# One layer of gated attention, one of window attention: full-width operands, moved copies and moved squares

## The chip, the cores and the metric

The kernel runs on one core of a Trainium2 chip. Its engines are TensorE (PE, matrix products; PEld is its load of weights), VectorE (DVE), ScalarE (ACT), GpSimd (POOL) and SyncE (SP, which only issues transfers). Each has its own instruction stream; they meet at semaphores. DMA queues are fed by SP and ACT (hardware queues) and by POOL (a software queue). The metric is the device time in microseconds of one execution, the median of the runs shown.

## What is computed

One inference step of a decoder of two layers for two groups of requests that share the weights: a prompt of 1024 tokens and 8 samples of 8 tokens, so 1088 token columns of 1024 features. Layer 0 mixes tokens with gated linear attention (four heads, keys of 128, values of 256 features), layer 1 with attention over a window of 128 positions, a bias table and past keys and values. Each layer then has an MLP with squared ReLU and a gated embedding:

```python
def step(state, inp):                       # linear attention, per head and chunk
    bc = jnp.cumsum(lc, axis=-2)            # lc = log_sigmoid(a @ w_a2 + b_a2) / 16
    attn = jnp.einsum('bhid,bhjd,bhijd->bhij', qc, kc, decay)
    o = (jnp.einsum('bhij,bhje->bhie', attn, vc)
         + jnp.einsum('bhid,bhde->bhie', qc * jnp.exp(bc), state))
    new_state = (jnp.exp(last)[..., None] * state
                 + jnp.einsum('bhjd,bhje->bhde', kc * jnp.exp(last - bc), vc))
...
h = h + gla_or_swa(rmsnorm(h, w['norm_mix'][i]))
h = h + jnp.square(jax.nn.relu(rmsnorm(h, w['norm_mlp'][i]) @ w_up)) @ w_down
gate = jax.nn.sigmoid(rmsnorm(h, w['norm_ple'][i]) @ w['w_ple_gate'][i])
h = h + gate * (p[i] @ w['w_ple'][i])
```

Outputs are the final activations, the new states of the linear attention and the key and value caches of the window (for the samples: the old cache moved on by eight positions).

## The kernel before

Activations lie with features on the 128 partitions and the 1088 tokens along the free dimension, in 8 tiles. Products run in three parts: weights and activations are split into a high part (rounded to fp32r) and the rest, and `mm3` (L163, L164, L165) adds high*high, high*rest and rest*high into one PSUM tile. Token columns come in three chunks (364, 362, 362), so one weight tile of 128x512 (four blocks of 128 features) serves 36 matmuls.

Weights come through `wfill`: a load into one of two `raw` buffers on SP's queue, a cast on ACT (L139, `whi`), a subtraction on DVE (L140, `wlo`), each into one of five buffers. `wnext` keeps this three tiles ahead of PE. `load()` (L77) issues on SP and chains every load behind the one before, so that SP's order is the order in which the program was written. The order on the other engines is set by a scheduler that goes by its own cost model and may put instructions of one engine in another order than they were written.

`gla_layer` first loads the eight input tiles x; per tile it makes the split (L195 on ACT, L196 on DVE) and sums the squares of x for the norm into `acc`: squares on ACT (L275) or POOL (L273), sums on DVE (L281, L283, L288) or POOL (L279). PE meanwhile multiplies tile after tile with the first head's q and k weights; then it sums `acc` over partitions (L231). After that the attention runs as a generator, `gla_steps`, over 4 heads x 9 chunks (8 of the prompt, one of the samples), with the projections of the next head filled in between its matmuls. The steps that the change touches:

- `gla_lg`: the gate's logarithm; L463 multiplies `aT` (17 rows: 16 features and a row of ones) with `wa2`, loaded anew for each head (17x128).
- `gla_scores`: scores of a chunk by levels of s = 64, 32, ..., 1; L534 takes `w-s` columns of E as weights, so 64 of them at s = 64 and 96 to 127 at the others. L536 and L537 follow.
- `gla_out`: L558, L563, L565 with full tiles.
- `gla_out_sample`: the samples' chunk; L594 multiplies `km` (masked keys, 64 rows) with `vs` (values, 64 rows), two passes for each of 8 samples' pairs, L599 multiplies `vs` with `ats` (64 rows).

An fp32 matmul shows as two passes in the trace (x2 for one matmul).

`bias_rows` at the layer's end makes 16 rows of 384 bias values in DRAM (`ed1`); `bias_copies` (L795, L798) spreads them to 16x128 rows (`ed`) in eight copies of 384 KB and copies the old caches (`kcs`, `vcs`, 960 KB each) to their place in the outputs. It is called at the start of each of the eight blocks (fb) of the first MLP. Its transfers are issued by POOL, where nothing else stands ahead of them, so that they start as soon as `ed1` is written, during the output projection of the attention (`out_proj`). `sample_bias` reads `ed` into `bs`, and the window attention reads both.

`out_proj` adds to each of its products the residual, which is loaded again from the input into one single buffer x (L659, on ACT's queue); the sum is DVE's (L640), then follow squares for the next norm (L225, L226) and splits. `mlp` runs over 8 blocks: four up tiles f (each of two weight tiles, three chunks; evacuated by L691 on DVE, L692 and L693 on ACT, L694 on DVE) and then eight down tiles.

Of the kernel before, what the change touches and what calls it, by code (L numbers as in the profile page):

```python
# [19 lines left out]
P = 128  # L20
D = 1024
KT = D // P
# [24 lines left out]
class Trunk:  # L47
# [204 lines left out]
    def gla_layer(self):  # L252
        nc, I, O = self.nc, self.I, self.O
        with ExitStack() as ctx:
# [4 lines left out]
            for k in range(KT):  # L259
                x = self.single()  # L260
                if k == 0:
                    self.wfill(1)
                for c0, cn in CH if k == 0 else ((0, T),):
                    self.load(x[:, c0:c0 + cn], I["xT"][k][:, c0:c0 + cn])
                self.wfill((2, 2, 2, 3, 4, 4, 5, 5)[k])
                self.split(hg[k], x, self.gain(G_MIX0, k), CH if k == 0 else ((0, T),))

                if k == 0:
                    nc.scalar.activation(self.acc[:, :T], x, AF.Square)
                    continue  # L270
                sq = self.double("G3", F32, [P, T])
                if k in (1, 4):
                    nc.gpsimd.tensor_tensor(sq, x, x, op=ALU.mult)  # L273
                elif k < KT - 1:
                    nc.scalar.activation(sq, x, AF.Square)  # L275
                if k == 1:
                    acc2 = sq
                elif k in (3, 4):
                    nc.gpsimd.tensor_tensor(acc2, acc2, sq, op=ALU.add)  # L279
                elif k < KT - 1:  # L280
                    nc.vector.tensor_tensor(self.acc[:, :T], self.acc[:, :T], sq, op=ALU.add)  # L281
                if k == 6:
                    nc.vector.tensor_tensor(self.acc[:, :T], self.acc[:, :T], acc2, op=ALU.add)  # L283
                if k == KT - 1:
                    for c0, cn in CH:
                        c = slice(c0, c0 + cn)
                        nc.scalar.activation(sq[:, c], x[:, c], AF.Square)
                        nc.vector.tensor_tensor(self.acc[:, c], self.acc[:, c], sq[:, c], op=ALU.add)  # L288
            self.norm_end(token_major=True)

            self.load(self.ident, I["ident"])
            self.load_wa2(0)
            tri = ga.tile([P, P], F32R, name="tri")
# [21 lines left out]
            for a in self.at:  # L315
                nc.gpsimd.memset(a, 0.0)
            self.ats = ga.tile([TS, TS], F32, name="ats")
            nc.gpsimd.memset(self.ats, 0.0)
# [35 lines left out]
    def gla_proj(self, h, hg):  # L354
# [26 lines left out]
        v = d["v"] = self.double("G3", F32, [P, 8, DV])  # L381
        vs = d["vs"] = self.ga.tile([TS, DV], F32, tag="vs", name=self.uid("vs"), bufs=1)
        wv = [self.wnext(("v", h, g)) for g in range(4)]
# [14 lines left out]
        if h == 0:  # L398
            aT = self.aT = self.rs.tile([P, TP], F32, tag="acc", name="aT", bufs=1)
            nc.gpsimd.memset(aT[:17, :], 1.0)  # L400
            for t0 in range(0, 9, 4):
# [51 lines left out]
    def gla_lg(self, h, c):  # L453

        nc, ga = self.nc, self.ga
        if c == 0:
            self.wa2 = self.wa2next
            if h + 1 < HEADS:
                self.load_wa2(h + 1)
        m, n = (P, 2) if c < 8 else (TS, 1)  # L460
        ps = self.ps("gs")
        for i in range(n):
            nc.tensor.matmul(ps[:m, i * P:(i + 1) * P], lhsT=self.aT[:17, (c + i) * P:(c + i) * P + m],  # L463
                             rhs=self.wa2, start=True, stop=True)
        w = n * P
# [10 lines left out]
                                                 for i in range(n)}}  # L476

    def load_wa2(self, h):
        self.wa2next = self.ga.tile([17, P], F32, tag="wa2", name=self.uid("wa2"), bufs=2)
        self.load(self.wa2next, self.I["wa2"][h])  # L480

# [40 lines left out]
    def gla_scores(self, h, c, pre):  # L522
# [8 lines left out]
        for l, s in enumerate(levels):  # L531
            ev = E[:, l, :].rearrange("p (n two s) -> p n two s", two=2, s=s)
            nc.vector.tensor_tensor(ev, ev, _dims(base, ([2 * s, w // (2 * s)], [T + s, 2], [1, s])), op=ALU.mult)
            nc.tensor.matmul(pp[:w - s, l * hw:(l + 1) * hw], lhsT=E[:, l, :w - s], rhs=ev[:, :, 1, :], start=True, stop=True)  # L534
        nc.vector.tensor_tensor(ke[:, :w], ke[:, :w], base, op=ALU.mult)
# [40 lines left out]
    def gla_out_sample(self, h, st):  # L576
        nc, ga, g, d = self.nc, self.ga, self.g, self.head[h]
        pp, pd, kt, qe, sm = st
        vs, o, tok = d["vs"], d["o"], SEQ
        self.gla_pick(self.ats, g["msks"], pp, pd, TS, LVS)  # L580
        pi = self.ps("gx")
        for b in range(NB):
            if b % 2 == 0:
                km = ga.tile([TS, 2, P], F32, tag="km", name=self.uid("km"), bufs=1)
                nc.vector.tensor_tensor(km, kt[:TS, :].unsqueeze(1).broadcast_to([TS, 2, P]),
                                        g["bmask"][:, b:b + 2].unsqueeze(2).broadcast_to([TS, 2, P]), op=ALU.mult)
                pu = self.ps("gs")
# [202 lines left out]
    def bias_copies(self, i):  # L790
# [3 lines left out]
        s = slice(2 * i, 2 * i + 2)  # L794
        r = self.nc.gpsimd.dma_start(self.ed[s], self.ed1[s].unsqueeze(1).broadcast_to([2, P, 384]))  # L795
        if i == FB - 1:
            for out, past in (("kcs", "kpast"), ("vcs", "vpast")):
                c = self.nc.gpsimd.dma_start(self.O[out][:, 0:120, :], self.I[past][:, 8:128, :])  # L798
                self.order(c.ins, r.ins)

# [450 lines left out]
```

## Time and profile before

| | before |
|---|---|
| median of 3 runs | 2784.34 us (2783.4 to 2785.63) |
| profiled execution | 2783.81 us |
| its span | 2782.0 us |
| PE busy | 2743.9 us, 99% |
| DVE / ACT / POOL busy | 52% / 38% / 5% |

The span is what the trace covers; a little lies around it. Matmuls are pipelined: their durations overlap, so the distance from start to start is what one costs. In a shape like 64*128 64x256 the first pair is the weights' rows and columns, the second the moving operand's rows and columns. What stands in brackets at a row's end is how long the engine was idle before it, and who ended that.

### The profile page before, as it was taken

Reading aid. Unit: us, or ns where it says so; the run is one execution under the profiler, and the core shown is the slowest. Engines: PE = TensorE matmul, PEld = TensorE weight load, DVE = VectorE, ACT = ScalarE, POOL = GpSimd, SP = SyncE. Lnnn points to the kernel's source line nnn. Section 1 sums busy time; section 2 is a strip of 40 time slices with the busy share of each in tenths; the row PEclk is TensorE's granted clock in tenths of the full one; section 3 lists DMA queues with packets and bytes.
Section 4 is the critical chain, followed back from the end, with each engine's and each line's share of the span. In section 5 each row is a group of like instructions: output and inputs, shape, how many; then the busy total and the mean of one; then the engine's idle time right before and its main releaser. Section 6 shows DMA issues by size and latency. Waiting matters only on the chain.

```text
span 2782.0 us, 43335 instructions
## 1 busy us (share of the span) xinstructions
PE 2743.9 (99%) x17265; PEld 2655.9 (95%) x17265; DVE 1455.3 (52%) x3479; ACT 1058.6 (38%) x2301; POOL 148.2 (5%) x166
## 2 busy tenths in 40 slices
PE   8999999999999999999999999999999999999997
PEld 8988988999999999999999988799999999999997
DVE  5766876543333333333756577654333333333687
ACT  4544655432221221122534566533222221221475
POOL 1000000040000000000000233200000000000000
PEclk9999999999999999999999999999999999999999
DMA  3111121341111111111122101121111111111053
GB/s 116 35 59 39 31 69 58 114 118 46 46 54 42 55 43 45 46 42 43 54 71 82 48 24 54 55 79 50 42 54 45 43 51 46 46 46 42 24 192 101
DMA packets 96322, 163.40 MB, mean 59 GB/s; under 512 B 16457, under 2 KB 33501, under 8 KB 96088
## 3 DMA queue, kind: packets, MB, share of 16 engines
q1 hardware_dynamic: 87448, 150.09, 17.8%
q0 software_dynamic: 7520, 6.09, 0.8%
q10 hardware_dynamic: 1152, 4.46, 0.5%
q8 instruction: 136, 2.23, 0.3%
q14 instruction: 66, 0.54, 0.1%
HBM read 145.94 MB, written 19.98 MB: 60 GB/s over the span
## 4 chain that ended last, share of the span: by engine, by line
PE 95%; DVE 2%; ACT 1%; DMA 1%; issue 1%; SPq 0%; POOL 0%; DVEq 0%; ACTq 0%; POOLq 0%
PE mm L163 21%; PE mm L164 21%; PE mm L165 21%; PE gx L165 7%; PE gx L164 7%; PE gx L163 7%; PE gx L534 2%; PE gx L1024 1%; PE gx L1010 1%; PE gs L594 1%; PE gx L563 1%; DMA x<-in_xT 1%; PE gx L558 1%; PE gs L993 1%; PE gx L592 0%
## 5 line engine op out<-in xcount | busy, mean ns | idle before, releaser
L163 PE MATMUL mm<-G,whi 128*128 128x362 f32 (+1 forms) x3416 | 1130.6, 331 | 6.6 <-ACT G L195 6.2
L164 PE MATMUL mm<-G,whi 128*128 128x362 f32 (+1 forms) x3416 | 1127.8, 330 | 2.4 <-DVE G L196 2.4
L165 PE MATMUL mm<-G,wlo 128*128 128x362 f32 (+1 forms) x3416 | 1126.7, 330 | 0.1
L163 PEld LDWEIGHTS mm<-G,whi 128*128 128x128 f32 x3416 | 642.8, 188 | 15.6 <-ACT G L195 6.5
L164 PEld LDWEIGHTS mm<-G,whi 128*128 128x128 f32 x3416 | 643.2, 188 | 9.0 <-issue 3.6
L165 PEld LDWEIGHTS mm<-G,wlo 128*128 128x128 f32 x3416 | 642.4, 188 | 5.8 <-issue 3.5
L139 ACT CAST whi<-raw 128x512 fp32r<-128x512 f32 (+1 forms) x368 | 226.8, 619 | 722.7 <-PE mm L164 702.9
L165 PE MATMUL gx<-G,wlo 128*128 128x362 f32 (+1 forms) x1048 | 343.6, 328 | 1.3 <-DVE wlo L140 1.3
L164 PE MATMUL gx<-G,whi 128*128 128x362 f32 (+1 forms) x1048 | 343.7, 328 | 0.0
L163 PE MATMUL gx<-G,whi 128*128 128x362 f32 (+1 forms) x1048 | 343.0, 328 | 0.0
L140 DVE TENSOR_TENSOR wlo<-raw,whi 128x512 fp32r<-128x512 f32 (+1 forms) x368 | 257.6, 702 | 68.1 <-ACT whi L139 67.2
L703 DVE TENSOR_TENSOR H<-H,mm 128x364 f32<-128x364 f32 (+1 forms) x256 | 136.2, 532 | 271.2 <-PE mm L165 269.9
L692 ACT ACTIVATE tmp<-tmp 128x362 f32<-128x362 f32 (+1 forms) x192 | 97.3, 508 | 392.6 <-DVE tmp L691 385.5
L165 PEld LDWEIGHTS gx<-G,wlo 128*128 128x128 f32 x1048 | 197.5, 188 | 1.8 <-DVE wlo L140 1.6
L163 PEld LDWEIGHTS gx<-G,whi 128*128 128x128 f32 x1048 | 197.5, 189 | 0.1
L164 PEld LDWEIGHTS gx<-G,whi 128*128 128x128 f32 x1048 | 197.3, 188 | 0.1
L694 DVE TENSOR_TENSOR G<-tmp,G 128x362 fp32r<-128x362 f32 (+1 forms) x192 | 102.9, 537 | 166.1 <-ACT G L693 166.1
L691 DVE SCALAR_TENSOR_TENSOR tmp<-mm,rb 128x364 f32<-128x364 f32 (+1 forms) x128 | 68.6, 536 | 178.4 <-PE mm L165 178.4
L703 DVE TENSOR_TENSOR H<-H,gx 128x362 f32<-128x362 f32 x128 | 68.0, 531 | 140.9 <-PE gx L165 140.9
L225 ACT ACTIVATE tmp<-H 128x362 f32<-128x362 f32 (+1 forms) x126 | 63.6, 506 | 143.8 <-DVE H L640 85.4
L925 POOL TENSOR_TENSOR G<-tmp,G 64x364 fp32r<-64x364 f32 (+2 forms) x48 | 45.0, 939 | 983.7 <-ACT G L924 976.2
L693 ACT CAST G<-tmp 128x362 fp32r<-128x362 f32 (+1 forms) x192 | 95.1, 496 | 5.9
(247 smaller groups left out, 3066.5 us busy)
## 6 DMA issues: line engine op xcount, KB each, us to landing
raw<-in_w_up SPq DMA_DIRECT2D x128, 256.0 KB, 2.6
raw<-in_w_down SPq DMA_DIRECT2D x128, 256.0 KB, 2.6
G<-in_w_gate SPq DMA_DIRECT2D x24, 512.0 KB, 3.6
raw<-in_w_o SPq DMA_DIRECT2D x32, 256.0 KB, 3.2
raw<-in_w_q SPq DMA_DIRECT2D x24, 256.0 KB, 2.7
x<-in_xT ACTq DMA_DIRECT2D x8, 544.0 KB, 6.6
hd<-H SPq DMA_DIRECT2D x8, 544.0 KB, 3.8
x<-hd SPq DMA_DIRECT2D x8, 544.0 KB, 3.6
```

The costliest lines, as they stand in the source:

```text
L139: nc.scalar.copy(hi[:, s], raw[:, s])
L140: nc.vector.tensor_tensor(lo[:, s], raw[:, s], hi[:, s].bitcast(F32), op=ALU.subtract)
L163: mm(out, lhsT=w[0], rhs=x[0], start=first, stop=False)
L164: mm(out, lhsT=w[0], rhs=x[1], start=False, stop=False)
L165: mm(out, lhsT=w[1], rhs=x[0], start=False, stop=last)
L225: nc.scalar.activation(sq[:, :cn], h[:, s], AF.Square)
L534: nc.tensor.matmul(pp[:w - s, l * hw:(l + 1) * hw], lhsT=E[:, l, :w - s], rhs=ev[:, :, 1, :], start=True, stop=True)
L691: nc.vector.scalar_tensor_tensor(t[:, :cn], ps, 0.0, rb[:, s], op0=ALU.max, op1=ALU.mult)
L692: nc.scalar.activation(t[:, :cn], t[:, :cn], AF.Square)
L693: nc.scalar.copy(u[:, 0, s], t[:, :cn])
L694: nc.vector.tensor_tensor(u[:, 1, s], t[:, :cn], u[:, 0, s].bitcast(F32), op=ALU.subtract)
L703: nc.vector.tensor_tensor(h[:, s], h[:, s], ps, op=ALU.add)
```

## The change

Three things are changed.

1. Operands of the linear attention get 128 rows. `wa2` is one tile of 128 rows for all heads, set to zero on POOL and loaded once in its first 17 rows; `aT` is set to one in all 128 rows; `vs`, `km` and `ats` are tiles of 128 rows that are set to zero once, and later writes go to their first 64 rows. So L463, L594 and L599 contract over 128 rows. In `gla_scores` the weights of a level with 64 columns become w columns (128 at s = 64 of the prompt's chunks, 64 in the samples' chunk).
2. The copies of `bias_copies` are issued by `load()`, on SP's queue, in the order of the loads.
3. In the start the squares of all input tiles are ACT's, and their sums are DVE's.

```diff
@@ gla_layer
-                if k in (1, 4):
-                    nc.gpsimd.tensor_tensor(sq, x, x, op=ALU.mult)
-                elif k < KT - 1:
+                if k < KT - 1:
                     nc.scalar.activation(sq, x, AF.Square)
-                if k == 1:
-                    acc2 = sq
-                elif k in (3, 4):
-                    nc.gpsimd.tensor_tensor(acc2, acc2, sq, op=ALU.add)
-                elif k < KT - 1:
                     nc.vector.tensor_tensor(self.acc[:, :T], self.acc[:, :T], sq, op=ALU.add)
-                if k == 6:
-                    nc.vector.tensor_tensor(self.acc[:, :T], self.acc[:, :T], acc2, op=ALU.add)
...
-            self.load_wa2(0)
+            self.wa2 = ga.tile([P, HEADS, P], F32, name="wa2")
+            nc.gpsimd.memset(self.wa2, 0.0)
+            self.load(self.wa2[:17], I["wa2"].rearrange("h r c -> r h c"))
+            self.vs = ga.tile([P, DV], F32, name="vs")
+            self.km = ga.tile([P, 2, P], F32, name="km")
+            nc.gpsimd.memset(self.vs, 0.0)
+            nc.gpsimd.memset(self.km, 0.0)
...
-            self.ats = ga.tile([TS, TS], F32, name="ats")
+            self.ats = ga.tile([P, TS], F32, name="ats")
@@ gla_proj
-        vs = d["vs"] = self.ga.tile([TS, DV], F32, tag="vs", name=self.uid("vs"), bufs=1)
+        vs = self.vs[:TS]
...
-            nc.gpsimd.memset(aT[:17, :], 1.0)
+            nc.gpsimd.memset(aT, 1.0)
@@ gla_lg
-        if c == 0:
-            self.wa2 = self.wa2next
-            if h + 1 < HEADS:
-                self.load_wa2(h + 1)
...
-            nc.tensor.matmul(ps[:m, i * P:(i + 1) * P], lhsT=self.aT[:17, (c + i) * P:(c + i) * P + m],
-                             rhs=self.wa2, start=True, stop=True)
+            nc.tensor.matmul(ps[:m, i * P:(i + 1) * P], lhsT=self.aT[:, (c + i) * P:(c + i) * P + m],
+                             rhs=self.wa2[:, h, :], start=True, stop=True)
@@ gla_scores
-            nc.tensor.matmul(pp[:w - s, l * hw:(l + 1) * hw], lhsT=E[:, l, :w - s], rhs=ev[:, :, 1, :], start=True, stop=True)
+            m = w - s if w - s > 64 else w
+            nc.tensor.matmul(pp[:m, l * hw:(l + 1) * hw], lhsT=E[:, l, :m], rhs=ev[:, :, 1, :], start=True, stop=True)
@@ gla_out_sample
-        vs, o, tok = d["vs"], d["o"], SEQ
-        self.gla_pick(self.ats, g["msks"], pp, pd, TS, LVS)
+        vs, km, o, tok = self.vs, self.km, d["o"], SEQ
+        self.gla_pick(self.ats[:TS], g["msks"], pp, pd, TS, LVS)
...
-                km = ga.tile([TS, 2, P], F32, tag="km", name=self.uid("km"), bufs=1)
-                nc.vector.tensor_tensor(km, kt[:TS, :].unsqueeze(1).broadcast_to([TS, 2, P]),
+                nc.vector.tensor_tensor(km[:TS], kt[:TS, :].unsqueeze(1).broadcast_to([TS, 2, P]),
@@ bias_copies
-        r = self.nc.gpsimd.dma_start(self.ed[s], self.ed1[s].unsqueeze(1).broadcast_to([2, P, 384]))
+        self.load(self.ed[s], self.ed1[s].unsqueeze(1).broadcast_to([2, P, 384]))
...
-                c = self.nc.gpsimd.dma_start(self.O[out][:, 0:120, :], self.I[past][:, 8:128, :])
-                self.order(c.ins, r.ins)
+                self.load(self.O[out][:, 0:120, :], self.I[past][:, 8:128, :])
```

The order on the engines at three places. First DVE in the start, while PE multiplies the input tiles; G is the split of a tile where H is read, else a square. Before:

```order
L196 SCALAR_TENSOR_TENSOR G_85<-H_116,gains,G_85 128x1088
L196 SCALAR_TENSOR_TENSOR G_86<-H_122,gains,G_86 128x1088
L281 TENSOR_TENSOR acc_92<-acc_92,G_126 128x1088
L196 SCALAR_TENSOR_TENSOR G_87<-H_129,gains,G_87 128x1088
L140 TENSOR_TENSOR wlo_134<-raw_131,whi_133 128x512
L196 SCALAR_TENSOR_TENSOR G_88<-H_142,gains,G_88 128x1088
L140 TENSOR_TENSOR wlo_147<-raw_144,whi_146 128x512
L196 SCALAR_TENSOR_TENSOR G_89<-H_155,gains,G_89 128x1088
L281 TENSOR_TENSOR acc_92<-acc_92,G_159 128x1088
```

And now:

```order
L196 SCALAR_TENSOR_TENSOR G_85<-H_116,gains,G_85 128x1088
L273 TENSOR_TENSOR acc_92<-acc_92,G_120 128x1088
L196 SCALAR_TENSOR_TENSOR G_86<-H_123,gains,G_86 128x1088
L273 TENSOR_TENSOR acc_92<-acc_92,G_127 128x1088
L140 TENSOR_TENSOR wlo_135<-raw_132,whi_134 128x512
L196 SCALAR_TENSOR_TENSOR G_87<-H_130,gains,G_87 128x1088
L273 TENSOR_TENSOR acc_92<-acc_92,G_140 128x1088
L140 TENSOR_TENSOR wlo_148<-raw_145,whi_147 128x512
L196 SCALAR_TENSOR_TENSOR G_88<-H_143,gains,G_88 128x1088
L273 TENSOR_TENSOR acc_92<-acc_92,G_153 128x1088
```

Behind every split of a tile there stands now an addition (after's L273). Second, ACT in the first MLP at the end of a block's first up tile, whose three chunks are squared and cast by L692 and L693. Before:

```order
L139 CAST whi_7333<-raw_7331 128x512
L139 CAST whi_7382<-raw_7380 128x512
L139 CAST whi_7388<-raw_7386 128x512
L692 ACTIVATE tmp_7418<-tmp_7418 128x364
L693 CAST G_7392<-tmp_7418 128x364
L692 ACTIVATE tmp_7448<-tmp_7448 128x362
L693 CAST G_7392<-tmp_7448 128x362
L139 CAST whi_7485<-raw_7483 128x512
L139 CAST whi_7491<-raw_7489 128x512
L692 ACTIVATE tmp_7478<-tmp_7478 128x362
L693 CAST G_7392<-tmp_7478 128x362
```

And now, with those lines as L681 and L682:

```order
L139 CAST whi_7312<-raw_7310 128x512
L681 ACTIVATE tmp_7397<-tmp_7397 128x364
L682 CAST G_7371<-tmp_7397 128x364
L681 ACTIVATE tmp_7427<-tmp_7427 128x362
L682 CAST G_7371<-tmp_7427 128x362
L681 ACTIVATE tmp_7457<-tmp_7457 128x362
L682 CAST G_7371<-tmp_7457 128x362
L139 CAST whi_7361<-raw_7359 128x512
L139 CAST whi_7367<-raw_7365 128x512
L139 CAST whi_7464<-raw_7462 128x512
L139 CAST whi_7470<-raw_7468 128x512
```

The cast of the second up tile's second half (7382 before, 7361 now) has moved behind the three pairs. PE has moved with it: before it took both halves of the second tile chunk by chunk (24 matmuls each); now it takes the first half for all three chunks, 12 matmuls each, and then the second half. It is so in each of the eight blocks. Third, SP in the last block of the first MLP; before, only loads of weights stood there, and POOL had the copies, in this order:

```order
L785 DMA ed_5484<-rows 16x384
L795 DMA ed<-ed_5484 256x1x384 x8
L798 DMA out_kcs<-in_kpast 8x2x15360
L798 DMA out_vcs<-in_vpast 8x2x15360
L815 DMA bs<-ed 32x1x128
```

Now SP has:

```order
L77 DMA raw_12054<-in_w_up 128x512
L77 DMA raw_12102<-in_w_up 128x512
L77 DMA ed<-ed_5463 256x1x384
L77 DMA out_kcs<-in_kpast 8x2x15360
L77 DMA out_vcs<-in_vpast 8x2x15360
L77 DMA raw_12153<-in_w_up 128x512
L77 DMA raw_12159<-in_w_up 128x512
```

In the other seven blocks one copy of `ed` stands between two loads of up weights. Behind the first MLP the order of PE, ACT and DVE is as before.

## Rows read from the trace of the kernel before

**Rows 1.** The page, chain that ended last: shares of the span by engine.

```profile
PE 95%; DVE 2%; ACT 1%; DMA 1%; issue 1%; SPq 0%; POOL 0%; DVEq 0%; ACTq 0%; POOLq 0%
```

**Rows 2.** Windows: length; busy PE, PEld, DVE, ACT, POOL (instructions); clock; DMA; GB/s.

```profile
45.00:485.00 440.00, 439.52 (x3017) 398.57 (x3016) 301.72 (x1103) 230.82 (x596) 2.35 (x4) 1.00 0.15 47
...
603.80:607.20 3.40, 3.40 (x10) 2.87 (x11) 3.40 (x8) 1.62 (x5) 3.40 (x7) 0.50 0.12 9
```

**Rows 3.** Timeline of PE, 81.1 to 83.0: start, us, line, operands, shapes, count.

```profile
81.10 0.53 PE L534 MATMUL gx<-E 128*112 128x64 f32 x4
81.47 0.28 PE L537 MATMUL gx<-ident,ke 128*128 128x128 f32 x1
81.68 0.33 PE L534 MATMUL gx<-E 128*64 128x64 f32 x2
...
82.21 0.33 PE L164 MATMUL mm<-G,whi 128*128 128x362 f32 x1
82.38 0.59 PE L558 MATMUL gx<-G,kt 128*128 128x256 f32 x2
...
82.97 0.33 PE L163 MATMUL mm<-G,whi 128*128 128x362 f32 x1
```

**Rows 4.** Timeline of PE, 158.1 to 159.4, around one L594.

```profile
158.12 0.32 PE L165 MATMUL mm<-G,wlo 128*128 128x364 f32 x1
158.38 0.70 PE L594 MATMUL gs<-vs,km 64*128 64x256 f32 x2
...
159.27 0.33 PE L164 MATMUL mm<-G,whi 128*128 128x364 f32 x1
```

**Rows 5.** Timeline of PE, 71.0 to 72.4, around one L463.

```profile
71.02 0.33 PE L165 MATMUL mm<-G,wlo 128*128 128x364 f32 x1
71.28 0.71 PE L463 MATMUL gs<-wa,aT 17*128 17x128 f32 x4
...
72.19 0.33 PE L164 MATMUL mm<-G,whi 128*128 128x364 f32 x1
```

**Rows 6.** Groups of PE by shape, 45 to 485: count, busy us, mean ns.

```profile
L594 PE MATMUL gs<-vs,km 64*128 64x256 f32 x64 | 22.3, 428 | 0.0
...
L463 PE MATMUL gs<-wa,aT 17*128 17x128 f32 x64 | 11.8, 299 | 0.0
...
L534 PE MATMUL gx<-E 128*64 128x64 f32 x64 | 10.5, 246 | 0.0
```

**Rows 7.** Waits of PE, 0 to 45: us in total, times, longest us.

```profile
PE mm L164 <- DVE G L196: 2.4, 2, 1.5
PE gx L165 <- DVE wlo L140: 1.3, 1, 1.3
PE gs L231 <- DVE acc L288: 1.2, 1, 1.2
```

**Rows 8.** Timeline of DVE, 20 to 27.

```profile
20.33 3.00 DVE L140 TENSOR_TENSOR wlo<-raw,whi 128x512 fp32r<-128x512 f32 x1
...
24.52 0.68 DVE L140 TENSOR_TENSOR wlo<-raw,whi 128x512 fp32r<-128x512 f32 x1
25.12 1.34 DVE L196 SCALAR_TENSOR_TENSOR G<-H,gains,G 128x1088 fp32r<-128x1088 f32 x1
```

**Rows 9.** Transfers issued in 486 to 625: queue, count, KB, us to landing.

```profile
out_vcs<-in_vpast POOLq DMA_DIRECT2D x1, 960.0 KB, 16.9
```

**Rows 10.** Line L659, the residual's loads: times to landing.

```profile
DMA to landing us min/median/max: 4.4/6.6/8.8
```

**Rows 11.** Timelines of DVE and of PE, 594 to 605.

```profile
596.27 0.54 DVE L640 TENSOR_TENSOR H<-mm,x 128x364 f32<-128x364 f32 x1 [7.86 <-DMA x<-in_xT]
...
603.63 1.43 PE L231 MATMUL gs<-acc,ones 128*128 128x362 f32 x2 [1.92 <-DVE acc L226]
```

**Rows 12.** Timeline, 711.5 to 713.6: one chunk's evacuation in the first MLP.

```profile
711.88 0.53 DVE L691 SCALAR_TENSOR_TENSOR tmp<-mm,rb 128x362 f32<-128x362 f32 x1 [0.82 <-PE mm L165]
...
712.99 0.49 ACT L693 CAST G<-tmp 128x362 fp32r<-128x362 f32 x1
```

More of the change, by code (lines that the diff above doesn't have):

```diff
@@ L476, in gla_lg @@
                                                  for i in range(n)}}
-    def load_wa2(self, h):
-        self.wa2next = self.ga.tile([17, P], F32, tag="wa2", name=self.uid("wa2"), bufs=2)
-        self.load(self.wa2next, self.I["wa2"][h])
     def c128(self, s):
```

## The prediction

> **What bounds the kernel now.** I read the chain of waits first: TensorE (PE) makes up 95% of it [rows 1], so a microsecond leaves the time only if PE's own steps shorten or a stretch in which PE stands idle gets shorter. The windows come next, one for each stage that the diff touches. In the linear attention, 45 to 485 us, PE is busy for 439.52 of 440.00 us [rows 2]: there are no waits to win there, only steps of PE. In the start, 0 to 45 us, and at the end of the attention's output projection, 580 to 605 us, PE does wait, and the timelines of those places are read for who is late. The changed kernel's order of instructions tells what moves.
>
> **Part 1, operands of 128 rows (and L534's last level of 128 columns).** The number of instructions stays the same; what is in question is their step. The timeline of PE shows starts; a matmul of the projections (L163 to L165, 362 columns) steps by 0.17 us, and PE's time for an inserted group is read from the start of the matmul ahead of it to the start of the second one behind it.
> The nearest full group is L558, two passes of 256 columns with 128 rows and 128 columns: 82.21 to 82.97, 0.76 us [rows 3]. L594 streams the same two passes of 256 columns, but with 64 rows: 158.12 to 159.27, 1.15 us [rows 4]. The difference, 0.39 us, can't be a wait for data, because the rows name no releaser. L463 streams four passes of 128 columns, 512 columns as well, with 17 rows: 71.02 to 72.19, 1.17 us [rows 5], or 0.41 over the full group. L534's last level has 128 rows but only 64 columns of weights: from L537's start at 81.47 to 82.21 is 0.74 us [rows 3]. Its full neighbours, four passes of the 112-column level, go from 81.10 to 81.47, 0.09 each, so L537, two passes and the next L163 should take about 0.11 + 0.18 + 0.17 = 0.46: 0.28 too much.
> Counts by shape [rows 6]: L594 x64 passes is 32 groups of two, L463 17*128 x64 is some 18 groups (thirteen of four, the rest of two, estimated), L534 128*64 x64 is 32 groups of two.
> - L594: 32 x 0.39 = 12.4 as the upper end. Where L592 or L534 stand beside it the groups share their change of shape with a neighbour that is full; I take 11.5.
> - L463: 18 x 0.41 = 7.4; I take 7.2. Its four matmuls in the samples' chunk (17*64) become 128*64 and stay half a tile in columns, so I count nothing for them.
> - L534: 32 x 0.28 = 9.0 as the upper end, 0 as the lower: the row also holds the change from transposes (L537), which stays. I take 5, nearer to the row than to nothing.
> - L599, one matmul pair in each of the four heads, with 64 rows like L594: at most 4 x 0.39, taken as 0.3 because three of the four follow L594 and share its change of shape.
> Sum 24.0 us, bounds 17 (nine tenths of the first two, nothing for the third) and 29 (all upper ends). More rows cost VectorE and ScalarE nothing: the tiles are zeroed once by GpSimd, which is idle for most of the span, and the later writes cover the same 64 or 17 rows as before. The three later loads of the gate's weights vanish from SP's queue; PE waits for no load here [rows 2], so that is worth nothing.
> The Trainium skill, "TensorE: Matmul & The Clock Gate", section "Why this matters for your kernels", says that a single matmul of 32 rows takes the same time as one of 128; by it the rows of L594 and L463 would bring nothing and part 1 would be 5 us instead of 24. "TensorEngine Tiling (Array Packing)", section "Key Properties", says that a change of the tiling mode drains the engine; by that rule 0.39 us beside each short group is what goes. The rows side with the second.
>
> **Part 2, the input's squares without GpSimd.** Before, PE waits in 0 to 45 us for VectorE three times in kind: 1.3 for L140, 2.4 for L196 and 1.2 for L288 [rows 7], 4.9 us in all. (PE's wait for ScalarE's L195 is the first load's arrival, and stays.) VectorE is late because its steps stretch: the same L140 takes 3.00 us at 20.33 and 0.68 us at 24.52 [rows 8], after GpSimd has ended its squares and sums. Now VectorE has six additions of 1088 columns where it had four, 2 x 1.3 us more if one takes what L196 takes at that size (1.34 at 25.12), and no GpSimd work beside them: the one stretched L140 alone gives back 2.3 us, and three other steps between 8.8 and 20.3 us are stretched alike. VectorE then needs about 1.3 + 1.3 + 0.7 = 3.3 us for an input tile with a weight tile and 2.6 for one without, against 18 x 0.166 = 3.0 us of PE; on average it keeps up, by little. ScalarE gets two squares more; only L195's wait for the first load is charged to it there. I take the whole 4.9 us; bounds 3 (VectorE is late once or twice) and 5.5 (a short stretch of half clock behind the last wait goes too).
>
> **Part 3, copies on SP among the first MLP's loads.** In the output projection GpSimd's queue copies 8 x 384 KB and 2 x 960 KB. The last, out_vcs, is under way for 16.9 us [rows 9], across the load of the last residual tile x, whose kind lands in 4.4 to 8.8 us [rows 10]. VectorE stands 7.86 us for it, its additions end late, and PE waits 1.92 us at 603.63 [rows 11]; behind that wait PE's granted clock is 0.50 (the 1.2 GHz level of its two) for 3.40 us [rows 2], half of which, 1.70, is lost. With the copies gone, an x that lands in 4.4 instead of 8.8 comes 4.4 us earlier, more than 1.92, so wait and slow clock can both go: 3.6. It may also be VectorE's splits of the finished tiles in the same place that are late next, so I take 3.2, bounds 0 and 3.6.
> The price is in the first MLP. SP issues the copy ahead of the up weights of each of the eight blocks; the order shows that ScalarE's casts of the second up tile's second half now stand behind the three squares and casts of the first tile, and that PE therefore does the first half of the sum of all three column chunks (36 matmuls, 36 x 0.166 = 6.0 us) before the second. The squares end 1.6 us after L691 starts (711.88 to 712.99 + 0.49), then a cast and an L140 of 0.68, the cast taken as long: the weights are ready about 3.0 us into these 6.0 us [rows 8, 12]. In blocks 2 and 4 a cast of the layer's embedding (1088 columns) and its subtraction stand there too; at twice the width of a weight tile I put them at 2 us more, still under 6.0. The loads: weights are fetched three tiles ahead of use, some 18 us at 6.0 us a tile, and one 384 KB copy ahead of them is shorter than the 16.9 us that 960 KB takes [rows 9]. I cost part 3's new place at 0; without that cover each block would cost its stall and 1.7 us of half clock. Bound: 0 to 4 us more.
>
> **Sum.** The profiled execution took 2783.8 us against a median of 2784.3, and its span is 2782.0; what lies around the span is not touched. 2783.8 - 24.0 - 4.9 - 3.2 = 2751.7, so 2752 us. Bounds: 2783.8 - 29 - 5.5 - 3.6 = 2745.7, and 2783.8 - 17 - 3 - 0 = 2763.8; with 4 us in the MLP it would be 2768.
>
> **Rivals.**
> - *The short rows are not what costs* (the change does not do what it says). The extra 0.39 would belong to the place, not to the shape: a change of PSUM bank or of the operand's type, which zeros don't take away. For it speaks that L534, with full rows, shows 0.28 as well; against it that L558 changes type and bank alike and shows nothing. Then L594 and L463 bring 0 and the time is 2783.8 - 5 - 4.9 - 3.2 = 2771. This is also what the rule of a time that doesn't depend on rows would give. Chance 0.10.
> - *Only the tiles pay.* VectorE is as late as before with its two additions more, or the last x tile is held up by the weight loads that run at the same time: 2783.8 - 24 = 2760. For it speaks that VectorE's 3.3 us per tile is above PE's 3.0 where a weight tile falls in. Chance 0.14.
> - *Slower: the first MLP stalls.* If the copies hold up the up weights, or the second half's weights come more than 6.0 us after the first tile's end, PE stops once in each block and starts again at half clock. It decides from the point where the stall passes 6.0 us of cover; to eat up the 32 us it takes 4.0 us for each of eight blocks, a stall of 2.3 and 1.7 of clock. With a stall of 3.5 each it is 2752 + 8 x 5.2 = 2793. Against it speak the 3 us of slack above and the three tiles of lead. Chance 0.04.
>
> **How the numbers follow.** My forecast has 0.68, the three rivals 0.10, 0.14 and 0.04, and 0.04 is for what I don't see, half of it near no change. The range 2745 to 2764 holds the forecast with its bounds and the second rival, 0.82. About 0.2% (5.6 us) is what a measurement of this kernel can tell from no change: every case but the third rival and the rest lies below that, so faster 0.92, same 0.04, slower 0.04.
>
> **What would show it.** In the profile after, PE's starts around L594's and L463's successors should be 0.76 apart where they were 1.15 and 1.17, and PE's work that filled 45 to 485 us should fill 24 us less; if it is 5 us less, the first rival holds. In 0 to 45 us PE's waits for VectorE should be gone, and no VectorE step of 1088 should take over 1.4 us. At the end of the output projection PE should pass to the MLP without a wait at the norm and without a stretch of clock 0.50; if the x tile still comes late, the second rival holds there. In the first MLP PE should be busy throughout; a wait of PE for the casts or subtractions of the up weights, eight times, would be the third rival, and would make the forecast wrong.

## The result

The changed kernel takes 2755.1 us in the median (2752.8 to 2755.6) where the kernel before takes 2783.9 (2780.9 to 2785.6): the ratio is 0.990 with an interval of 0.988 to 0.991, so 28.7 us less by the medians. The forecast was 2752, the range 2745 to 2764. In a later series seven runs of the kernel before have a median of 2789.0 (2779.8 to 2795.2) and four of the changed kernel 2755.1, 33.8 us less: the kernel before varies more from run to run than the changed one.

The page of the profiled execution after (2754.8 us): its span, PE's busy time, and the chain that ended last.

```profile
span 2753.0 us, 43316 instructions
...
PE 2720.5 (99%) x17265; PEld 2657.6 (97%) x17265; DVE 1446.2 (53%) x3481; ACT 1057.7 (38%) x2303; POOL 128.0 (5%) x155
...
PE 95%; DVE 2%; ACT 1%; DMA 1%; issue 0%; POOL 0%; DVEq 0%; SPq 0%; ACTq 0%; POOLq 0%
```

PE bounds the kernel as before [rows 1], with the same number of matmuls. Where the time went is read from PE's starts at four fixed places: the first product of the values (`mm<-whi,G`), the first transpose of the gate's features (`gs<-ident,atok`), the bias table's product (`gs<-rows,tab`), and PE's matmul 4,200 (counted from 0), early in the first MLP. The attention's stage lies between the second and the third; these are its windows, first before, then after (columns as in rows 2):

```profile
68.91:484.02 415.11, 414.63 (x2823) 374.36 (x2820) 297.68 (x1095) 224.34 (x577) 2.35 (x4) 1.00 0.16 48
```

```profile
64.68:459.72 395.04, 392.83 (x2823) 375.00 (x2820) 296.67 (x1095) 224.11 (x577) 2.31 (x4) 1.00 0.17 50
...
590.00:1345.00 755.00, 755.00 (x4542) 754.15 (x4541) 307.66 (x549) 196.02 (x358) 27.47 (x48) 1.00 0.19 54
```

The same 2823 matmuls take 20.1 us less, and PE is now idle for 2.2 us of them where it was for 0.5. In the first MLP (last row) PE is busy throughout: the copies cost nothing there. The first value product starts 4.3 us earlier (37.67 against 41.97), and the stretch from the bias table's product to matmul 4,200 is 4.2 us shorter (166.83 against 171.01). Together that is 28.5 of the 29.0 us between the two spans.

What remains of PE's waits in 0 to 590 us (total, times, longest):

```profile
PE mm L163 <- ACT G L195: 6.0, 2, 5.2
PE gx L581 <- DMA s<-in_st: 0.7, 1, 0.7
PE gs L481 <- DVE tmp L205: 0.4, 1, 0.4
PE gs L481 <- ACT lgh L466: 0.3, 2, 0.2
...
```

The three waits of [rows 7] and the 1.92 us of [rows 11] are gone; new are the wait for the samples' states s and those of L481 (L492 of before): one for L205, the first step of a head's output norm, and two short ones for the cast of the gate's logarithm, `lgh`.

The groups of [rows 4] and [rows 5] after, timelines of PE:

```profile
150.97 0.33 PE L165 MATMUL mm<-G,wlo 128*128 128x364 f32 x1
151.15 0.59 PE L583 MATMUL gs<-vs,km 128*128 128x256 f32 x2
151.39 0.51 PE L163 MATMUL mm<-G,whi 128*128 128x364 f32 x1
151.74 0.32 PE L164 MATMUL mm<-G,whi 128*128 128x364 f32 x1
...
66.79 0.33 PE L165 MATMUL mm<-G,wlo 128*128 128x364 f32 x1
66.96 0.61 PE L456 MATMUL gs<-wa,aT 128*128 128x128 f32 x4
...
67.58 0.33 PE L164 MATMUL mm<-G,whi 128*128 128x364 f32 x1
```

150.97 to 151.74 is 0.77 us where it was 1.15; 66.79 to 67.58 is 0.79 where it was 1.17. Both now cost about what L558's full group costs in [rows 3], 0.76.

### The profile page after: what moved, and what is told of

It is laid out like the page before. It is cut to its first block, busy times and chain, and to the rows that moved or that the text cites. A ratio compares the mean times of both kernels' runs of the same rounds, so it can differ in the third digit from the quotient of the medians.

```text
span 2753.0 us, 43316 instructions
## 1 busy us (share of the span) xinstructions
PE 2720.5 (99%) x17265; PEld 2657.6 (97%) x17265; DVE 1446.2 (53%) x3481; ACT 1057.7 (38%) x2303; POOL 128.0 (5%) x155
## 4 chain that ended last, share of the span: by engine, by line
PE 95%; DVE 2%; ACT 1%; DMA 1%; issue 0%; POOL 0%; DVEq 0%; SPq 0%; ACTq 0%; POOLq 0%
PE mm L163 21%; PE mm L164 21%; PE mm L165 21%; PE gx L165 7%; PE gx L164 7%; PE gx L163 7%; PE gx L524 2%; PE gx L1012 1%; PE gx L998 1%; PE gx L553 1%; PE gx L548 1%; PE gs L583 1%; PE gs L981 1%; PE gx L555 0%; PE gs L231 0%
## 5 line engine op out<-in xcount | busy, mean ns | idle before, releaser
L140 DVE TENSOR_TENSOR wlo<-raw,whi 128x512 fp32r<-128x512 f32 (+1 forms) x368 | 251.9, 691 | 67.7 <-ACT whi L139 67.0
L692 DVE TENSOR_TENSOR H<-H,mm 128x364 f32<-128x364 f32 (+1 forms) x256 | 136.2, 532 | 277.2 <-PE mm L165 276.0
L681 ACT ACTIVATE tmp<-tmp 128x362 f32<-128x362 f32 (+1 forms) x192 | 97.2, 507 | 462.5 <-DVE tmp L680 457.1
L692 DVE TENSOR_TENSOR H<-H,gx 128x362 f32<-128x362 f32 x128 | 68.0, 532 | 141.7 <-PE gx L165 141.7
L682 ACT CAST G<-tmp 128x362 fp32r<-128x362 f32 (+1 forms) x192 | 95.1, 496 | 5.8
L226 DVE TENSOR_TENSOR acc<-acc,tmp 128x362 f32<-128x362 f32 (+1 forms) x126 | 67.2, 535 | 36.2 <-ACT tmp L225 35.3
```

Of the source, the lines that this page charges most:

```text
L140: nc.vector.tensor_tensor(lo[:, s], raw[:, s], hi[:, s].bitcast(F32), op=ALU.subtract)
L226: nc.vector.tensor_tensor(self.acc[:, s], self.acc[:, s], sq[:, :cn], op=ALU.add)
L681: nc.scalar.activation(t[:, :cn], t[:, :cn], AF.Square)
L682: nc.scalar.copy(u[:, 0, s], t[:, :cn])
L692: nc.vector.tensor_tensor(h[:, s], h[:, s], ps, op=ALU.add)
```

## The experiments

The table puts all kernels together: PE's starts, worked out from the traces, in microseconds.

| kernel | first value product at | attention's stage | bias product to matmul 4,200 | 4,200 to 8,600 (MLP) |
|---|---|---|---|---|
| before | 41.97 | 415.11 | 171.01 | 731.78 |
| after | 37.67 | 395.04 | 166.83 | 731.81 |
| after, again | 37.57 | 394.36 | 166.83 | 731.81 |
| part 1 alone | 42.66 | 394.66 | 172.77 | 731.79 |
| part 2 alone | 38.52 | 415.41 | 169.43 | 731.78 |
| part 3 alone | 43.92 | 415.24 | 166.84 | 731.80 |
| L594, L599 alone | 43.63 | 403.81 | 170.24 | 731.77 |
| L463 alone | 41.75 | 411.37 | 169.28 | 731.80 |
| L534 alone | 42.37 | 410.22 | 174.31 | 731.78 |
| 96 rows | 41.74 | 394.67 | 172.00 | 731.77 |
| after, wide sums | 36.25 | 394.82 | 166.83 | 731.82 |
| after, wide sums, samples' chunk | 36.32 | 394.00 | 166.83 | 731.81 |
| after, early gate | 36.67 | 394.36 | 166.84 | 731.80 |

Two columns vary where a kernel's code there is that of before: the first value product from 41.7 to 43.9 (mean of seven 42.6), the projection's end from 169.3 to 174.3 (mean of seven 171.3). The attention's stage repeats within 0.7 us. What the table leaves out, from matmul 8,600 to the end of the span, holds code that no part touches and takes between 1392.7 us (part 1 alone) and 1397.0 (after, again); it is 1395.2 before and 1394.7 after. PE's granted clock is 0.50 there for up to 10.2 us in the window attention: 10.2 before, 6.8 after, none in part 1 alone and with 96 rows. So whole times differ by some 4 us for reasons outside the change, and what a part is worth is read from the stages. The medians show it too: beside the 2789.8 of before in one series (19 runs, 2780.9 to 2795.3) the three parts alone are 26.8, 12.6 and 7.2 us shorter, in sum more than the whole change (the ratios below are estimates with an interval, not quotients of these medians). Of the long runs of before no trace was kept, so where they lose their time is not known.

### Each part alone

Part 1 alone: `wa2`, `aT`, `vs`, `km`, `ats` and L534's columns as in the change, the rest as before.

> The kernel before with part 1 alone (operands of 128 rows, L534's last level of 128 columns). Theory (the short shapes are what costs, whatever else is changed): the attention from its first chunk to the projection's begin is as much shorter as in the changed kernel, 19.9 us by PE's starts, and the start and the projection's tail keep their waits: about 2783.9 - 20 = 2764 us. Rival (the tiles bring the forecast 24 us by themselves, and the other two parts take 4 back in the attention): 2760 us. Second rival (the shapes don't cost): above 2775 us.

Measured: 2763.0 us, ratio to before 0.991 (0.989 to 0.993). The attention's stage is 20.4 us shorter, as in the changed kernel, so the theory holds and the rivals fall: the other parts take nothing back in the attention. That 2763.0 is so near to the forecast 2764 is in part luck: in the profiled execution the projection's end took 1.8 us more than before and the stretch behind matmul 8,600 2.5 us less. What is missing against the forecast's 24 is missing within part 1.

The start in this kernel is the old one, and shows more than the profile of before did. DVE and PE, timelines of part 1 alone:

```profile
18.69 3.03 DVE L140 TENSOR_TENSOR wlo<-raw,whi 128x512 fp32r<-128x512 f32 x1
21.64 3.57 DVE L196 SCALAR_TENSOR_TENSOR G<-H,gains,G 128x1088 fp32r<-128x1088 f32 x1
25.13 0.68 DVE L140 TENSOR_TENSOR wlo<-raw,whi 128x512 fp32r<-128x512 f32 x1
...
25.26 0.44 PE L164 MATMUL mm<-G,whi 128*128 128x364 f32 x1 [3.17 <-DVE G L196]
```

PE waits 3.17 us in one piece for the two stretched steps, and then a stretch at half clock follows (25.30 to 29.50 has a mean granted clock of 0.65):

```profile
25.30:29.50 4.20, 4.20 (x17) 4.20 (x18) 4.20 (x5) 3.39 (x6) 0.00 (x0) 0.65 0.70 194
```

Part 2 alone:

```diff
-                if k in (1, 4):
-                    nc.gpsimd.tensor_tensor(sq, x, x, op=ALU.mult)
-                elif k < KT - 1:
+                if k < KT - 1:
                     nc.scalar.activation(sq, x, AF.Square)
...
+                    nc.vector.tensor_tensor(self.acc[:, :T], self.acc[:, :T], sq, op=ALU.add)
```

> The kernel before with part 2 alone (no squares or sums on GpSimd in the start). Theory: PE's three kinds of wait for VectorE in 0 to 45 us go (4.9 us), and the thin matmuls L244, which then follow the norm's L231 closely, are followed by a stretch of clock 0.50 of about 3 us that gives 1.6 us back: the attention's first value product starts 4.3 us earlier, 2779.5 us. Rival (the stretch of clock 0.50 in the changed kernel comes from the other parts): no such stretch, 5 to 6 us earlier, 2778 us.

Measured: 2777.2 us, ratio 0.9965 (0.995 to 0.998); the first value product at 38.5, 3.4 us earlier than before where 4.3 were expected. Its trace has the slow stretch: 34 to 39 us at a mean clock of 0.66, behind L244. So the theory's pattern is there, but the next experiments show that it is not there in every run. The steps of DVE in the changed kernel:

```profile
15.31 0.69 DVE L140 TENSOR_TENSOR wlo<-raw,whi 128x512 fp32r<-128x512 f32 x1
15.91 1.35 DVE L196 SCALAR_TENSOR_TENSOR G<-H,gains,G 128x1088 fp32r<-128x1088 f32 x1
17.17 1.28 DVE L273 TENSOR_TENSOR acc<-acc,G 128x1088 f32<-128x1088 f32 x1
```

Nothing is stretched any more, against [rows 8]; this is the place of the 3.00 us.

Part 3 alone:

```diff
-        r = self.nc.gpsimd.dma_start(self.ed[s], self.ed1[s].unsqueeze(1).broadcast_to([2, P, 384]))
+        self.load(self.ed[s], self.ed1[s].unsqueeze(1).broadcast_to([2, P, 384]))
...
-                c = self.nc.gpsimd.dma_start(self.O[out][:, 0:120, :], self.I[past][:, 8:128, :])
-                self.order(c.ins, r.ins)
+                self.load(self.O[out][:, 0:120, :], self.I[past][:, 8:128, :])
```

> The kernel before with part 3 alone (copies on SP in the first MLP). Theory: the wait of 1.92 us for the norm at the end of the output projection and the 3.40 us of clock 0.50 behind it are gone, 3.6 to 4.2 us; PE is busy throughout the first MLP: 2780 us. Rival (the tail's gain came from the attention's end falling otherwise, or the MLP stalls): within 1 us of the kernel before.

Measured: 2782.6 us, ratio 0.998 (0.997 to 0.999). The projection's stretch takes 166.84 us, like every kernel with the copies on SP to 0.01 us, and the MLP loses nothing. Queue and place were changed together: whether the copies on SP's queue during the projection would hold x up as well was not tried. This kernel's start came late in the profiled execution (43.92), with code there that is not changed; this, not the copies, makes up the 2 us between its span and what the theory says.

### The tiles one by one

```diff
 # L594 and L599 alone: vs, km, ats of 128 rows
 # L463 alone: wa2 and aT of 128 rows
 # L534 alone:
+            m = w - s if w - s > 64 else w
-            nc.tensor.matmul(pp[:w - s, ...], lhsT=E[:, l, :w - s], rhs=ev[:, :, 1, :], ...)
+            nc.tensor.matmul(pp[:m, ...], lhsT=E[:, l, :m], rhs=ev[:, :, 1, :], ...)
 # 96 rows: as part 1, with the operands of L463, L594 and L599 cut to 96 rows
+                nc.tensor.matmul(pu[...], lhsT=km[:96, i, :], rhs=vs[:96], start=True, stop=True)
```

> The kernel before with 128 rows for L594 and L599 alone. Measured is the attention's stage, from PE's first transpose of the gate's features (gs<-ident,atok) to the bias table's product (gs<-rows,tab), 415.1 us before and 20.1 to 20.5 less with all tiles. Theory (each group pays for its own change of shape): 11 to 12 us less, and L594's groups between projection matmuls step in 0.76. Rival (the terms share their changes of shape, so that one alone wins little): under 8 us.

> The kernel before with 128 rows for L463 alone. Theory: 6 to 7.2 us less in the attention's stage, no new wait. Rival: under 4 us, because the late loads of the gate's weights or a later wait take some back.

> The kernel before with 128 columns for L534's level of 64 alone. Theory (half the columns cost a change of shape like half the rows): 4 to 5.5 us less in the attention's stage. Rival (only rows cost; the 0.28 us at L537 belong to the transposes): under 1 us.

> The tiles of part 1 with 96 rows instead of 128 in L463, L594 and L599, L534 as in the change; the other parts as before. Theory (what costs is the step from an operand of up to 64 rows to one of more, not the number of rows that are left out): 96 rows do as well as 128, 20 us less in the attention's stage. Rival (it costs whenever rows are left out): 5 us less, what L534 brings.

Measured in the attention's stage (one execution each; 2771.0, 2778.0, 2782.4 and 2761.8 us beside 2786.7 of before): L594 and L599 11.3 us less, L463 3.7, L534 4.9; the sum is 19.9, and together they bring 20.1 to 20.7. So the terms add up. L463 is the one that falls short; the rival of its expectation, a later wait, is followed below. With 96 rows the stage is 20.4 us shorter, as with 128. The counts by shape of that kernel:

```profile
L592 PE MATMUL gs<-vs,km 96*128 96x256 f32 x64 | 19.5, 386 | 0.0
...
L465 PE MATMUL gs<-wa,aT 96*128 96x128 f32 x64 | 10.3, 278 | 0.0
```

A pass of L594 takes 386 ns here, 385 in the changed kernel with 128 rows, and 428 before [rows 6]. Rows left out are not what costs; the step from 64 (or 17) rows to more is. Nor is it the single pass. In three heads L599's four passes stand right behind L594's two; here is one of them, before and with L594 and L599 alone (there L597 and L602):

```profile
254.73 0.33 PE L164 MATMUL mm<-G,whi 128*128 128x364 f32 x1
255.00 0.70 PE L594 MATMUL gs<-vs,km 64*128 64x256 f32 x2
255.53 0.55 PE L599 MATMUL gx<-ats,vs 64*128 64x64 f32 x4
...
256.29 0.33 PE L163 MATMUL mm<-G,whi 128*128 128x364 f32 x1
```

```profile
253.86 0.33 PE L164 MATMUL mm<-G,whi 128*128 128x364 f32 x1
254.03 0.60 PE L597 MATMUL gs<-vs,km 128*128 128x256 f32 x2
254.46 0.55 PE L602 MATMUL gx<-ats,vs 128*128 128x64 f32 x4
...
255.07 0.33 PE L163 MATMUL mm<-G,whi 128*128 128x364 f32 x1
```

1.56 us become 1.21: the six short passes lost 0.35 together, no more than two alone. The price is paid once for a run of short passes.

L463 alone was compared with before group by group (matmuls between two projection matmuls; the 162 groups of the stage are the same in both). Of the 18 groups of L463 with 128 columns, twelve lose 0.38 to 0.40 us, in sum 4.7; the six others lose 0.8 together. Five of them stand behind L492 or L493, one ahead of the samples' L492, whose 64 rows stay. And ten later groups take 0.1 to 0.3 us longer, 1.8 in sum. Eight of the ten hold L492 or L493; in three of these, 0.5 us in sum, L492 starts as soon as a step of the gate's chain ends (DVE L470), in the others the trace names other steps or none. One of the six, first before, then with L463 alone (its L486 is L492, its L461 L463):

```profile
386.43 0.39 ACT L473 CAST lgh<-lge 128x256 fp32r<-128x256 f32 x1
386.54 0.32 PE L164 MATMUL mm<-G,whi 128*128 128x362 f32 x1
386.88 0.33 PE L492 MATMUL gs<-tri,lgh 128*128 128x128 f32 x1
387.14 0.71 PE L463 MATMUL gs<-wa,aT 17*128 17x128 f32 x4
387.77 0.43 PE L165 MATMUL mm<-G,wlo 128*128 128x362 f32 x1
```

```profile
382.67 0.39 ACT L471 CAST lgh<-lge 128x256 fp32r<-128x256 f32 x1
383.12 0.33 PE L486 MATMUL gs<-tri,lgh 128*128 128x128 f32 x1 [0.16 <-ACT lgh L471]
383.28 0.66 PE L461 MATMUL gs<-wa,aT 128*128 128x128 f32 x4
383.69 0.41 PE L165 MATMUL mm<-G,wlo 128*128 128x362 f32 x1
```

From the group's first start to the next projection matmul it is 0.89 us before and 0.57 after, a gain; but L486 starts only when the gate's logarithm is cast (ACT L471, until 383.06). Before, it was so already: the cast ends at 386.82 and L492 starts at 386.88, 0.34 behind the matmul ahead of it where 0.16 is usual. That wait hardly shows as idle time, because the matmul ahead counts as busy until 386.86. From the previous L463 to the end of the cast it is 3.52 us before (from 383.30) and 3.42 with L463 alone (from 379.64): the chain of ScalarE and VectorE steps sets the pace here, and it hardly got shorter with PE. In the changed kernel, in another head, the cast (ACT L466) ends at 184.03 and L481 starts at 184.08.

### The thin sums, and more of the same

The changed kernel's start has a stretch of half clock that before's profile did not have: the nine products L244, 18 passes with one column, and then matmuls at the 1.2 GHz level.

```profile
34.60:37.40 2.80, 2.80 (x11) 2.80 (x11) 2.59 (x8) 2.09 (x6) 0.30 (x1) 0.50 0.17 65
```

```diff
-                nc.tensor.matmul(ps[:, t:t + 1], lhsT=self.acc[:, t * P:(t + 1) * P], rhs=self.ones[:, 0:1],
+                nc.tensor.matmul(ps[:, t * 56:(t + 1) * 56], lhsT=self.acc[:, t * P:(t + 1) * P], rhs=self.ones[:, :56],
```

> The changed kernel with the token-wise norm sums (L244) done with 56 equal columns for each of the nine products instead of one; one of the 56 is read. Steps of these matmuls were 0.11 us at one column and are 0.09 to 0.11 at 64 and 128, so they should take no longer. Theory (the thin matmuls bring the stretch of clock 0.50 at 34.4 to 37.4 us): the stretch is gone and the kernel is 1.6 us faster than the changed kernel, some 2753.5 us. Rival (the slow stretch follows from all the fp32 matmuls there, or from something else): it stays, 2755 us.

> The changed kernel once more, beside the two others of this call. 2753 to 2756 us; the attention's stage (first transpose of the gate's features to the bias table's product) 395.0 us, the first value product at 36 to 38 us.

Measured: 2752.5 us for the wide sums, 2755.1 for the changed kernel again, in a later series. The wide sums have no such stretch. But the changed kernel, again, has none either:

```profile
30.00:45.00 15.00, 15.00 (x107) 14.04 (x106) 9.96 (x24) 6.70 (x18) 1.06 (x1) 1.00 0.24 73
```

With one column the stretch behind L244 stands in three of eleven traces (after, part 2 alone, part 3 alone), with 56 columns in none of two. That settles nothing. In the run without it the first input's second piece came 0.7 us later (PE's second matmul at 7.37 instead of 6.67) and the first value product stood at 37.57 all the same. Whether the thin passes bring the slow stretch stays open, and the 1.7 us of the wide kernel are within what starts differ by.

```diff
 # after, wide sums, samples' chunk
-        m, n = (P, 2) if c < 8 else (TS, 1)
+        m, n = (P, 2) if c < 8 else (P, 1)
-            tris = ga.tile([TS, TS], F32R, name="tris")
+            tris = ga.tile([P, TS], F32R, name="tris")
 # after, early gate: gla_lg(*steps[i + 2]) ahead of gla_scores instead of behind it
```

> The changed kernel with the norm sums of 56 columns (as in e4_wide) and, for the samples' chunk, L463's weights of 128 columns instead of 64 and L492's and L493's operands of 128 rows instead of 64 (zeros and ones added). The samples' groups of the changed kernel still show 0.28 to 0.52 us too much for L463 and 0.31 for L492 and L493, in each of the four heads. Theory (every operand of 64 rows or columns costs a change of shape): 2.4 us less in the attention's stage, with the 1.7 us in the start about 4 us less than the changed kernel. Rival (what is saved there turns into waits for the gate's chain, as after L463): under 1 us in the attention's stage.

> The changed kernel with the gate's chain (L463 and what follows it on ScalarE and VectorE) written ahead of a step's scores instead of behind them. Theory (L463 gives back about 1.8 us because the cast of the gate's logarithm now comes too late for L492): the waits of PE for that cast go, 1 to 2 us less in the attention's stage. Rival (the scheduler puts the chain in the same place, or the two operands' buffers are taken): no change.

Measured: 2754.4 and 2753.7 us beside 2755.1 of the changed kernel; the ranges overlap, so neither is shown to be faster. With the samples' chunk made full, each of its eight groups (L463, and L492 with L493, in four heads) loses 0.31 to 0.34 us, 2.6 in sum, as the theory says. The stage gains 0.4. What was saved came back in other groups, the rival's size but not its mechanism: the waits for the gate's cast are those of the changed kernel (0.3), and the largest is for the load of s, whose group takes 0.8 us longer. PE's waits in that kernel's attention, of which the first was 0.3 in the changed kernel beside it:

```profile
PE gx L582 <- DMA s<-in_st: 1.1, 1, 1.1
PE gx L554 <- DVE at L542: 0.5, 2, 0.4
PE gs L482 <- ACT lgh L467: 0.3, 2, 0.2
```

The early gate changes nothing in the stage (394.36 both), and the waits for the cast are still there (0.4 us in two), as the rival says. Writing the chain earlier did not make it earlier than PE needs it; why not was not followed further.

## Why the prediction was right, point by point

**The direction, the size and the range** came out: 28.7 us (33.8 in the later series) against 32, and the largest part of it where it was sought. The sum by stages (kernels with the part against those without, from the table) is 20.6 in the attention, 5.0 in the start and 4.5 at the projection's end, against 24.0, 4.9 and 3.2. That the sum is so near is in part luck: part 1 was put 3.4 too high and part 3 1.3 too low.

**Part 1, the step that was mis-sized.** L594 with L599 was taken as 11.8 and measures 11.3. L534 was taken as 5 and measures 4.9, but 5 was a choice between 0 and 9.0 and not worked out: 31 of the 32 groups lose 0.13 to 0.24, and the group of the row used loses 0.23, not the 0.28 that was read from it. L463 was taken as 7.2 and measures 3.7. The price per group was right for the twelve (0.39). The step that was wrong is "18 x 0.41" taken as gained in full: five of the groups stand behind L492 or L493, where no row had been read and where PE goes at the pace of the gate's chain, and later groups took 1.8 us back. The prediction took PE's 439.52 busy us of 440 [rows 2] to mean that there were only steps of PE and no waits. That does not follow: before, L492 at 386.88 starts at the end of its cast, and PE counts as busy all the same. In the changed kernel the groups that got shorter lose 23.6 us in sum, nearly the 24.0 of the forecast, and 3.8 us come back in others, 0.8 at the load of s and 0.6 at an L481 that waits for L205. The prediction named neither.

**The rival that the place costs and not the shape** falls: L463's and L594's places are unchanged, and with 128 rows, or with 96, their groups step in 0.77 to 0.79 us. The rule of the Trainium skill that a single matmul of 32 rows takes the time of one of 128 ("TensorE: Matmul & The Clock Gate", "Why this matters for your kernels") does not hold for a group that stands among full ones: the 0.39 us are there with 64 and with 17 rows (no run has 32). The runs fit to the Trainium skill's "TensorEngine Tiling (Array Packing)", "Key Properties", by which a change of the tiling mode drains the engine: a run of short passes pays once, whether it has two passes or six. That the short operands run in another mode, and that the 0.39 us are such a drain, no trace shows.

**Part 2** came out as worked out: no step of VectorE is stretched, PE's waits for it are gone, and six additions fit in. What the old start costs differs between executions: the first value product stands at 41.7 to 43.9 us in seven traces (part 1 alone: 3.17 us of wait at once, and half clock behind it), while the changed start has in some runs a slow stretch of its own. Taken over seven and four traces the gain is 5.0.

**Part 3** was right in mechanism and too small: 4.2 us against before's profile, above the bound of 3.6. The timeline of PE after has the norm's L231 following at once, 0.16 us behind the last product:

```profile
576.61 0.33 PE L165 MATMUL gx<-G,wlo 128*128 128x362 f32 x1
576.77 0.81 PE L231 MATMUL gs<-acc,ones 128*128 128x362 f32 x2
577.14 0.60 PE L163 MATMUL mm<-G,whi 128*128 128x362 f32 x1
```

The bound had 1.92 of wait and 1.70 of clock. It left out a small wait of PE earlier in the projection (0.4 us at 514, a step of 0.57 where 0.17 is usual) for the same kind of x tile, which is gone too. VectorE's waits for x fell from 30.8 us in eight to 12.1 in seven. [rows 10] was thinner than it reads: the trace has the landing of only two of the eight loads of x, and copies were under way beside both. In other runs of the old tail the loss is larger: in the trace with L534 alone it is 174.31 us for the stretch, 7.5 more than with the copies moved.

**The rival of the stalled MLP** fell, but its cover was used: ScalarE now waits there for the up weights' load, 25.8 us in thirteen waits where before has one of 0.3. ScalarE's waits there, and one of them in the changed kernel's timeline:

```profile
ACT whi L139 <- DMA raw<-in_w_up: 25.8, 13, 3.7
...
688.95 1.25 ACT L139 CAST whi<-raw 128x512 fp32r<-128x512 f32 x2 [2.90 <-DMA raw<-in_w_up]
```

PE does not notice: it is busy for 755.00 of 755 us there, with the tiles ahead.

## What to carry to other kernels

A small matmul among full ones is priced by what it does to its neighbours' starts, not by its own duration: compare the distance from the matmul ahead of it to the second one behind it with that of a full one that streams as many columns. Zeros that fill up an operand can be cheaper than leaving rows out. And when PE is busy for 99.9% of a stage, look at who released the matmuls that other engines feed, and how long before they started, since a wait shorter than the matmul ahead hardly shows as idle time. Here 3.8 of 23.6 us saved came back, and in a second step over two of 2.6.

## What was not expected of the hardware

- Operands of 96 rows cost as little as those of 128 (386 against 385 ns a pass for L594), those of 64 or 17 rows 0.39 us more for a group among full ones; 64 columns of weights instead of 128 cost 0.13 to 0.24 us a group. A run of six short passes costs no more than one of two.
- A pass of L244 with one column took 0.11 us (18 in 2.06), with 56 columns 0.12 (18 in 2.11): narrowing an fp32 product below that saved next to nothing.
- The copies, which took 12.7 to 16.9 us each on the software queue beside the loads of x, held up the up weights' loads on SP's queue (25.8 us of ScalarE's waits against 0.3 before; 25.4 with part 3 alone), and PE lost nothing by it: 731.81 us for the MLP against 731.78.
